# Dense stages in token blocks of 512, 256 and 288 columns instead of three of 352, and norms in pieces of at most 352

## The chip, the cores and the metric

The kernel runs on one core of one Trainium2 chip, as a single launch. The time is the device time of that launch in microseconds (us). The kernel before was timed in three runs: 2801.63, 2805.51 and 2806.05 us, with a median of 2805.51 us. One further execution was recorded by the hardware profiler; all rows below are of that execution.

The engines carry short names: PE is TensorE's matmul, PEld its weight load, DVE is VectorE, ACT is ScalarE, POOL is GpSimd and SP is SyncE.

## The reference

The kernel computes one step of a two-layer encoder trunk over 1056 tokens: 1024 of a prompt and 32 of a sample. The model width is 1024 and the hidden width of the feed-forward part is 2816.

```python
def rms_norm(x, g):
    y = xf * lax.rsqrt(jnp.mean(xf * xf, axis=-1, keepdims=True) + EPS)
    return (y * g.astype(jnp.float32)).astype(x.dtype)
...
    g = z @ w_glu + b_glu                     # end of the first mixer (S5)
    out = g[..., :D_MODEL] * jax.nn.sigmoid(g[..., D_MODEL:])
...
def conv_ffn(xn, conv_state, w_up, conv_w, conv_b, w_down):
    h = xn @ w_up
    a, bv = h[..., :D_FF], h[..., D_FF:]
    padded = jnp.concatenate([conv_state.astype(a.dtype), a], axis=1)
    c = conv_b + sum(conv_w[j] * padded[:, j:j + t] for j in range(CONV_W))
    out = (jax.nn.gelu(c) * bv) @ w_down
```

Each layer is x += mixer(rmsnorm(x)), then x += conv_ffn(rmsnorm(x)). The mixer of layer 0 is a diagonal state-space layer with a gated linear unit behind it. The mixer of layer 1 is an attention in which an indexer selects 256 keys for each query; it ends in a projection with attn_w_o.

## The kernel before

From the load of x into feature-major form on, the residual stays in one tile `xt`, with features on the 128 partitions and tokens along the columns. The input of a product is held in two float32r parts, `xh` and `xl`, whose sum is the normed value; each weight tile is likewise split into `whi` (by ACT, L143) and `wlo` (by DVE, L144). A product is therefore three matmuls for each tile of 128 features: L164 (whi times xh), L165 (whi times xl) and L166 (wlo times xh). The weight tile of 128x128 is the stationary operand, and the tokens are the moving columns. PSUM's tile for one product takes at most 512 columns.

The program's stages, with their places in the span, are the first mixer's recurrence (0 to 255 us), its gated linear unit `glu` (to about 473), `ffn` of layer 0 (to about 1244), the index scores, masks and projections of the second mixer (to about 1620), the attention (to about 1914), `out_proj` (to about 2022), and `ffn` of layer 1 with `store_block` (to the end). The stages with feature-major products, glu, out_proj and both ffn, are called the dense stages here. They cut the 1056 tokens in three blocks of `BLK = 352` columns, so that each weight tile meets each part of the input in three matmuls of 352 columns: 2688 in each of L164 to L166 for glu, the up products and out_proj, and 1056 in each for the down products, 11232 in all.

Between two stages stands the norm. `norm_block(b)` is called as soon as block b of `xt` is final, for each of three blocks in three places: glu to ffn 0, ffn 0 to the second mixer, and out_proj to ffn 1. ACT squares the eight feature tiles, DVE and POOL add them up (L193, L197), PE sums over partitions (L202, matmuls of one column), DVE forms the mean and, in some eleven small instructions, its inverse root (L173 to L178). PE then spreads that root over the partitions (L215), and DVE multiplies `xt` by it and by the gain (L218, eight times), ACT copies out `xh`, and DVE (five) and POOL (three) subtract for `xl` (L220). A product of the next stage can start on block b when these tiles are there.

Each engine works through its own list of instructions in order, and waits at semaphores for the others. A scheduler sets these lists when the kernel is built: it puts PE's norm instructions among the products of the neighbouring blocks, in the old stage and the new. If the instruction next in PE's list is L215 and DVE has not finished the root, PE waits, and the products behind it wait too.

`store_block(b)` turns the final `xt` of a block into rows of tokens: eight transposes on PE (L250), two copies on ACT (L251) and one DMA from SP for each tile of up to 128 tokens, with two `yrow` buffers. The blocks end at 352, 704 and 1056, so the tiles are 3, 3, 3 and the sample's one.

Of the kernel before, what the change touches and what calls it, by code (L numbers as in the profile page):

```python
# [23 lines left out]
BLK = 352  # L24
NB = T // BLK
# [24 lines left out]
class Trunk:  # L50
    """Shared tiles and helpers; the residual lives in xt[feature % 128, feature // 128, token]."""
# [43 lines left out]
    def load_vectors(self, pool):  # L95
        """Per-feature vectors, one column of 128 features each."""
# [34 lines left out]
    def weight(self, view, pool=False):  # L131
        """view [128, n] (rows on partitions): its two exact parts, as stationary operands; pool: split by the Pool engine."""
# [14 lines left out]
    def weight_rows(self, view, sh):  # L147
        """weight of a view whose rows lie apart."""
# [10 lines left out]
    def product(self, ps, terms):  # L159
        """ps += sum over (wh, wl, xh, xl) of w^T x, in float32 accuracy."""  # L160
# [8 lines left out]
    def rsqrt(self, y, m, tmp, iters=3):  # L169
        """y = m ** -0.5 elementwise; tmp: like y."""  # L170
# [9 lines left out]
    def norm_block(self, b, gname, g0):  # L180
        """xh/xl[:, :, block b] = parts of rmsnorm(xt) * gain."""
        nc = self.nc
        sl = slice(b * BLK, (b + 1) * BLK)
        # sums of squares, some tiles by the Pool engine
        acc = {}
        PA = (1, 3, 5)
        for k in range(KD):
            e = k in PA
            tag = "nsq" if e in acc else f"nacc{int(e)}"
            sq = self.sm.tile([P, BLK], F32, tag=tag, name=tag, bufs=self.nq if tag == "nsq" else 1)  # L190
# [9 lines left out]
        for j, o in enumerate(range(0, BLK, P)):  # L200
            n = min(P, BLK - o)
            nc.tensor.matmul(ps[:n, j : j + 1], acc[:, o : o + n], self.ones, start=True, stop=True)  # L202
        ms = self.sm.tile([P, 3], F32, tag="nms", name="nms")
        rs = self.sm.tile([P, 3], F32, tag="nrs", name="nrs")
        tm = self.sm.tile([P, 3], F32, tag="ntm", name="ntm")
        nc.vector.memset(ms, 1.0)
        for j, o in enumerate(range(0, BLK, P)):
            n = min(P, BLK - o)
# [4 lines left out]
        for j, o in enumerate(range(0, BLK, P)):  # L213
            n = min(P, BLK - o)
            nc.tensor.matmul(pb[:, o : o + n], rs[:n, j : j + 1].to_broadcast([n, P]), self.ident[:n, :n], start=True, stop=True)  # L215
        for k in range(KD):
            xn = self.sm.tile([P, BLK], F32, tag="nxn", name="nxn", bufs=self.nx)
# [21 lines left out]
    def store_block(self, pool, b):  # L239
        """y rows of block b."""  # L240
# [3 lines left out]
        e = min((b + 1) * BLK, TP)  # L244
        for o, n in [(o, min(P, e - o)) for o in range(b * BLK, e, P)] + ([(TP, TS)] if b == NB - 1 else []):
# [9 lines left out]
    def exp(self, pool, dst, x):  # L255
        """dst = exp(x) to float32 accuracy (range reduction, polynomial, exponent bits)."""
# [19 lines left out]
    def cmul(self, pool, orr, oi, xr, xi, yr, yi):  # L276
        """(orr + i oi) = (xr + i xi)(yr + i yi); shapes [.., s, n] already broadcast alike."""
# [44 lines left out]
    def ssm_params(self, pool, tmp, ld):  # L322
        """State-major tables of the discretized recurrence: partition = (re n | im n). The norm's gain is part of the inputs' taps."""
# [19 lines left out]
        # th = 2 pi k + (r + rl)  # L343
# [21 lines left out]
        # powers a^0 .. a^8  # L365
# [6 lines left out]
        # f = (a - 1) / lambda  # L372
# [22 lines left out]
        # rows to be transposed: 0-7 (Re af | Re af), 8-15 (-Im af | Im af), 16-23 (Re a | Re a),  # L395
        # 24-31 (-Im a | -Im a), 32 |a|^8, 33 state
# [24 lines left out]
        # turns per chunk of 8 tokens, in three parts  # L421
# [16 lines left out]
        # stationary rows (group | group): [0] parts 0 and 1, less a small shift; [1] part 0; [2] parts 1 and 2  # L438
# [13 lines left out]
        # input and output maps, state-major  # L452
# [63 lines left out]
        # the sample's rows take the place of b, c and the powers, which are of no more use  # L516
# [13 lines left out]
    def ssm(self):  # L530
        """xh + xl = gelu(S5(rmsnorm(x))), feature k*128 + g*16 + q at [q*8 + g, k]."""
        nc, I, O = self.nc, self.I, self.O
        C = 133  # chunk columns: 128 of the prompt, the sample's start state, 4 of the sample
        with ExitStack() as ctx:
# [34 lines left out]
            G0 = (0, 3, 6)  # groups are worked on three at a time  # L569
# [3 lines left out]
            def taps(o):  # L573
                """Input taps a^(7-j) f B, output taps C a^d, and |a|^8 of 8 groups."""
# [23 lines left out]
            def maps(o, d):  # L598
                """Within-chunk operands: inputs to state (re | im | re), inputs to outputs."""
# [25 lines left out]
            def angles(o, s):  # L625
                """cos and sin of the state's turns up to each chunk; the groups' inputs, [(j, cin), chunk]."""
# [1103 lines left out]
```

## Time and profile before

| | before |
|---|---|
| runs | 2801.63, 2805.51, 2806.05 us |
| median | 2805.51 us |
| span of the profiled execution | 2799.6 us |
| PE busy in the span | 2582.2 us (92%) |
| PEld busy | 2473.0 us (88%) |
| DVE busy | 1640.5 us (59%) |
| ACT busy | 976.6 us (35%) |
| POOL busy | 448.1 us (16%) |

The span runs from the first to the last instruction of the profiled execution; the runs' median lies 5.9 us above it. A busy share is an average over all stages, and a busy PE is not PE at its peak, since a matmul's record includes time in which the next one is already under way. A matmul's cost in a row of matmuls is therefore read from one start to the next, not from its mean duration.

### The profile page before, as it was taken

To read this page: it belongs to the slowest core of one execution; us is meant where nothing else is said; L and a number is where in the kernel's file an instruction comes from. 1 tells how busy PE (TensorE), PEld (TensorE's weight loads), DVE (VectorE), ACT (ScalarE), POOL (GpSimd) and SP (SyncE) were. 2 spreads that over 40 slices of the span, in tenths; PEclk is the share of its full clock that TensorE was granted. 3 is DMA by queue.
4 is the path that set the end of the run, shared out by engine and by line. 5 is a ranking of instruction groups with operands and counts; after the bars stand their busy time and mean duration, and the time that the engine had idled before them with its cause. 6 is when DMAs were issued, how large, how long until landed. Compare 5 with 4: busy or idle time off the path is not lost. (4 is left out here: it accounts for less than half of the span.)

```text
span 2799.6 us, 43287 instructions
## 1 busy us (share of the span) xinstructions
PE 2582.2 (92%) x17203; PEld 2473.0 (88%) x17203; DVE 1640.5 (59%) x3487; ACT 976.6 (35%) x1947; POOL 448.1 (16%) x696
## 2 busy tenths in 40 slices
PE   2887999999999999997986689999999999999999
PEld 2676999999999999996886667778999999999998
DVE  8886225644444444478799977663554444444443
ACT  4565213311111111134544466773331111111112
POOL 4672001100000000012144243220110000000000
PEclk9998999999999999998998889999999999999999
DMA  4334211111111111110121211212111111111111
GB/s 94 60 59 109 80 46 46 46 46 46 46 46 46 46 46 46 46 37 14 48 66 47 69 40 25 52 27 69 46 46 46 46 46 46 46 46 46 46 38 63
DMA packets 220662, 140.29 MB, mean 50 GB/s; under 512 B 50429, under 2 KB 212261, under 8 KB 220461
## 3 DMA queue, kind: packets, MB, share of 16 engines
q1 hardware_dynamic: 216733, 130.90, 17.0%
q10 hardware_dynamic: 3728, 6.64, 0.7%
q8 instruction: 135, 2.21, 0.3%
q14 instruction: 66, 0.54, 0.1%
HBM read 112.68 MB, written 13.40 MB: 45 GB/s over the span
## 5 line engine op out<-in xcount | busy, mean ns | idle before, releaser
L164 PE MATMUL ps_mm<-xh,whi 128*128 128x352 f32 x2688 | 870.4, 324 | 5.0 <-ACT whi L143 5.0
L166 PE MATMUL ps_mm<-xh,wlo 128*128 128x352 f32 x2688 | 869.6, 324 | 0.0
L165 PE MATMUL ps_mm<-xl,whi 128*128 128x352 f32 x2688 | 868.6, 323 | 0.0
L164 PEld LDWEIGHTS ps_mm<-xh,whi 128*128 128x128 f32 x2688 | 506.5, 188 | 5.3 <-ACT whi L143 5.2
L165 PEld LDWEIGHTS ps_mm<-xl,whi 128*128 128x128 f32 x2688 | 506.3, 188 | 0.0
L166 PEld LDWEIGHTS ps_mm<-xh,wlo 128*128 128x128 f32 x2688 | 506.0, 188 | 0.2 <-DVE wlo L144 0.2
L144 DVE TENSOR_TENSOR wlo<-wraw,whi 128x1024 fp32r<-128x1024 f32 (+1 forms) x145 | 175.5, 1222 | 416.4 <-ACT whi L143 416.4
L143 ACT CAST whi<-wraw 128x1024 fp32r<-128x1024 f32 (+1 forms) x145 | 149.9, 1047 | 712.1 <-PE ps_mm L165 702.3
L1603 DVE TENSOR_TENSOR xt<-xt,ps_mm 128x352 f32<-128x352 f32 x528 | 269.4, 520 | 191.5 <-PE ps_mm L166 191.4
L164 PE MATMUL ps_mm<-hh,whi 128*128 128x352 f32 x1056 | 341.0, 323 | 1.5 <-DVE xt L1603 1.5
L165 PE MATMUL ps_mm<-hl,whi 128*128 128x352 f32 x1056 | 340.9, 323 | 0.0
L166 PE MATMUL ps_mm<-hh,wlo 128*128 128x352 f32 x1056 | 340.7, 323 | 0.0
L1584 POOL COPY tails<-a 128x2 f32<-128x2 f32 x44 | 39.8, 904 | 1229.5 <-ACT a L1573 1229.5
L772 PE MATMUL ps_mm<-whi,xh 128*128 128x256 f32 (+3 forms) x560 | 165.8, 297 | 42.5 <-ACT raw L1217 42.5
L164 PEld LDWEIGHTS ps_mm<-hh,whi 128*128 128x128 f32 x1056 | 198.4, 188 | 2.1 <-DVE xt L1603 2.0
L166 PEld LDWEIGHTS ps_mm<-hh,wlo 128*128 128x128 f32 x1056 | 198.4, 188 | 0.0
L165 PEld LDWEIGHTS ps_mm<-hl,whi 128*128 128x128 f32 x1056 | 198.4, 188 | 0.0
L1591 DVE TENSOR_TENSOR c<-c,ps_mm 128x352 f32<-128x352 f32 (+2 forms) x176 | 71.5, 428 | 159.2 <-PE ps_mm L166 112.6
L774 PE MATMUL ps_mm<-whi,xl 128*128 128x256 f32 (+3 forms) x560 | 163.6, 293 | 0.0
L773 PE MATMUL ps_mm<-wlo,xh 128*128 128x256 f32 (+3 forms) x560 | 163.6, 293 | 0.0
L772 PEld LDWEIGHTS ps_mm<-whi,xh 128*128 128x128 f32 (+1 forms) x560 | 106.4, 190 | 47.4 <-ACT raw L1217 41.2
L1573 ACT COPY a<-ps_mm 128x352 f32<-128x352 f32 (+2 forms) x176 | 61.9, 378 | 242.1 <-PE ps_mm L166 242.0
(420 smaller groups left out, 3992.4 us busy)
## 6 DMA issues: line engine op xcount, KB each, us to landing
wraw<-in_ffn_w_up_dram SPq DMA_DIRECT2D x88, 512.0 KB
wraw<-in_ffn_w_down_dram SPq DMA_DIRECT2D x44, 512.0 KB
wraw<-in_ssm_w_glu_dram SPq DMA_DIRECT2D x128, 64.0 KB
wraw<-in_attn_w_in_dram SPq DMA_DIRECT2D x14, 512.0 KB
zo<-yo SPq DMA_DIRECT2D x64, 66.5 KB
xcm<-in_x_prompt_dram SPq DMA_DIRECT2D x8, 512.0 KB
cps<-cp SPq DMA_DIRECT2D x16, 256.0 KB
xrow<-in_x_prompt_dram ACTq DMA_DIRECT2D x8, 512.0 KB
```

The lines of the kernel that those rows point to most:

```text
L143: nc.scalar.copy(hi, raw)
L144: nc.vector.tensor_sub(lo, raw, hi.bitcast(F32))
L164: nc.tensor.matmul(ps, wh, xh, start=(i == 0), stop=False)
L165: nc.tensor.matmul(ps, wh, xl, start=False, stop=False)
L166: nc.tensor.matmul(ps, wl, xh, start=False, stop=(i == n - 1))
L772: self.nc.tensor.matmul(ps, xh, hi[:, c, a:b], start=(k == 0), stop=False)
L773: self.nc.tensor.matmul(ps, xh, lo[:, c, a:b], start=False, stop=False)
L774: self.nc.tensor.matmul(ps, xl, hi[:, c, a:b], start=False, stop=(k == KD - 1))
L1573: nc.scalar.copy(u["a"][:, co + 2 : co + 2 + n], ps[:, to - b * BLK : to - b * BLK + n])
L1584: nc.gpsimd.tensor_copy(tails[:, u["f"], 0:2], u["a"][:, TP : TP + 2])
L1591: nc.vector.tensor_mul(h, h, bv[:, to - b * BLK : to - b * BLK + n])
L1603: nc.vector.tensor_add(self.xt[:, m, blocks[b]], self.xt[:, m, blocks[b]], ps[:, :BLK])
```

## The change

The width of a block is no longer one number. `BLOCKS` lists the start and the width of each: 512, 256 and 288 columns. All dense stages take their columns from it. `norm_block(b)` now calls `norm_piece` for each of ceil(n / 352) equal pieces of the block: two of 256 columns for the first block, and one each for the others, so that a norm has four pieces instead of three. The tiles for the mean and its root have four columns instead of three. The stored tiles are 4, 2, 2 and 1.

```diff
-BLK = 352
-NB = T // BLK
+BLOCKS = [(0, 512), (512, 256), (768, 288)]
+NB = len(BLOCKS)
+BMAX = max(n for _, n in BLOCKS)
+NORM = 352
...
     def norm_block(self, b, gname, g0):
+        b0, n = BLOCKS[b]
+        c = -(-n // NORM)
+        for i in range(c):
+            self.norm_piece(b0 + i * n // c, n // c, gname, g0)
+
+    def norm_piece(self, b0, BLK, gname, g0):
         nc = self.nc
-        sl = slice(b * BLK, (b + 1) * BLK)
+        sl = slice(b0, b0 + BLK)
+        parts = [(j, o, min(P, BLK - o)) for j, o in enumerate(range(0, BLK, P))]
...
-            sq = self.sm.tile([P, BLK], F32, tag=tag, name=tag, bufs=self.nq if tag == "nsq" else 1)
+            sq = self.sm.tile([P, NORM], F32, tag=tag, name=tag, bufs=self.nq if tag == "nsq" else 1)[:, :BLK]
...
-        ms = self.sm.tile([P, 3], F32, tag="nms", name="nms")
+        ms = self.sm.tile([P, 4], F32, tag="nms", name="nms")
...
     def store_block(self, pool, b):
-        e = min((b + 1) * BLK, TP)
-        for o, n in [(o, min(P, e - o)) for o in range(b * BLK, e, P)] + ([(TP, TS)] if b == NB - 1 else []):
+        b0, n = BLOCKS[b]
+        e = min(b0 + n, TP)
+        for o, n in [(o, min(P, e - o)) for o in range(b0, e, P)] + ([(TP, TS)] if b == NB - 1 else []):
...
     def glu(self, after_block):
-                for b in range(NB):
-                    sl = slice(b * BLK, (b + 1) * BLK)
+                for b, (b0, BLK) in enumerate(BLOCKS):
+                    sl = slice(b0, b0 + BLK)
...
     def out_proj(self, after_block):
-            sl = slice(b * BLK, (b + 1) * BLK)
+            b0, BLK = BLOCKS[b]
+            sl = slice(b0, b0 + BLK)
...
     def ffn(self, layer, after_block, pool=None):
-        blocks = [slice(b * BLK, (b + 1) * BLK) for b in range(NB)]
+        blocks = [slice(o, o + n) for o, n in BLOCKS]
...
-                ps = self.ps()
-                self.product(ps[:, :BLK], [(w[0][:, k], w[1][:, k], self.xh[k][:, blocks[b]], self.xl[k][:, blocks[b]]) for k in range(KD)])
-                return ps[:, :BLK]
+                ps = self.ps()[:, : BLOCKS[b][1]]
+                self.product(ps, [(w[0][:, k], w[1][:, k], self.xh[k][:, blocks[b]], self.xl[k][:, blocks[b]]) for k in range(KD)])
+                return ps
```

The number of products does not change: 3744 matmuls of each of three widths where 11232 of one width stood. In the changed kernel the lines of `product` are L166 to L168, and the norm's two PE lines are L210 (sum over partitions) and L221 (spread of the root).

The scheduler's lists change around the norms. On PE, from glu to ffn 0 of the kernel before, the spread of block 1 has the sum of block 2 behind it (nrs is the root, nacc the sum of squares; xh, xl and whi, wlo are the parts of a product's operands):

```order
L164 MATMUL ps_mm<-xh,whi 128x352
L165 MATMUL ps_mm<-xl,whi 128x352
L215 MATMUL ps_aux<-ident,nrs 128x128 x2
L215 MATMUL ps_aux<-ident,nrs 128x96
L202 MATMUL ps_aux<-ones,nacc_4342 128x1 x2
L202 MATMUL ps_aux<-ones,nacc_4342 96x1
L166 MATMUL ps_mm<-xh,wlo 128x352
L164 MATMUL ps_mm<-xh,whi 128x352
```

The two products of 352 columns ahead of the spread, like those behind it, are some of the many that lie between the norm's rows here: 103 between the spreads of blocks 0 and 1, and 64 between those of blocks 1 and 2. In the kernel after, on PE at the same transition, this is the spread of the first block's second piece, with the sum of block 1 behind it:

```order
L166 MATMUL ps_mm<-xh,whi 128x288
L167 MATMUL ps_mm<-xl,whi 128x288
L168 MATMUL ps_mm<-xh,wlo 128x288
L221 MATMUL ps_aux<-ident,nrs 128x128 x2
L210 MATMUL ps_aux<-ones,nacc_4282 128x1 x2
L166 MATMUL ps_mm<-xh,whi 128x512
L167 MATMUL ps_mm<-xl,whi 128x512
L168 MATMUL ps_mm<-xh,wlo 128x512
```

Between the first piece's spread and this one stand 37 products of 288 columns, all of the old stage; the products of 512 columns behind it are the new stage's first, 30 of them up to the next spread and 47 from there to the last.

On DVE, at the same transition, the norm's wide instructions stand like this behind the first root (nxn is the normed tile, nms the mean, sg the gate of the old stage). Before:

```order
L178 SCALAR_TENSOR_TENSOR nrs<-ntm,nrs 128x3
L206 MEMSET nms 128x3
L218 SCALAR_TENSOR_TENSOR nxn<-xt,vec,ps_aux 128x352 x2
L220 TENSOR_TENSOR xl<-nxn,xh 128x352
L759 SCALAR_TENSOR_TENSOR sg<-ps_mm,vec,sg 128x352
L218 SCALAR_TENSOR_TENSOR nxn<-xt,vec,ps_aux 128x352 x2
L760 TENSOR_TENSOR xt<-xt,sg 128x352
L220 TENSOR_TENSOR xl<-nxn,xh 128x352
```

After:

```order
L214 MEMSET nms 128x4
L224 SCALAR_TENSOR_TENSOR nxn<-xt,vec,ps_aux 128x256 x2
L216 TENSOR_SCALAR nms<-ps_aux 128x1 x2
L202 TENSOR_TENSOR nacc_4282<-nacc_4282,nsq 128x256
L226 TENSOR_TENSOR xl<-nxn,xh 128x256
L175 TENSOR_SCALAR nrs<-nms 128x4
L224 SCALAR_TENSOR_TENSOR nxn<-xt,vec,ps_aux 128x256 x2
L176 TENSOR_SCALAR nrs<-nrs 128x4
```

The second piece's mean and root stand among the first piece's wide multiplications, and the sum of block 1's squares (nacc_4282) is already being formed there.

## Rows read from the trace of the kernel before

**Rows 1.** The page's head and its first part.

```profile
span 2799.6 us, 43287 instructions
PE 2582.2 (92%) x17203; PEld 2473.0 (88%) x17203; DVE 1640.5 (59%) x3487; ACT 976.6 (35%) x1947; POOL 448.1 (16%) x696
```

**Rows 2.** Costliest groups: line, engine, form, count | busy us, mean ns | idle before, releaser.

```profile
L164 PE MATMUL ps_mm<-xh,whi 128*128 128x352 f32 x2688 | 870.4, 324 | 5.0 <-ACT whi L143 5.0
L164 PE MATMUL ps_mm<-hh,whi 128*128 128x352 f32 x1056 | 341.0, 323 | 1.5 <-DVE xt L1603 1.5
```

**Rows 3.** Windows: length, then PE, PEld, DVE, ACT, POOL busy (count), clock, DMA share, GB/s.

```profile
455.00:560.00 105.00, 101.81 (x640) 100.39 (x639) 72.91 (x171) 42.05 (x86) 18.33 (x29) 1.00 0.14 41
560.00:1215.00 655.00, 655.00 (x4087) 655.00 (x4086) 305.26 (x489) 130.65 (x224) 23.74 (x72) 1.00 0.15 46
```

**Rows 4.** Timeline of PE, matmuls of other widths: start, duration, form [idle before].

```profile
1300.21 0.31 PE L773 MATMUL ps_mm<-wlo,xh 128*128 128x328 f32 x1
1302.93 0.31 PE L773 MATMUL ps_mm<-wlo,xh 128*128 128x328 f32 x1
...
1368.73 0.28 PE L772 MATMUL ps_mm<-whi,xh 128*128 128x256 f32 x1
1370.73 0.28 PE L774 MATMUL ps_mm<-whi,xl 128*128 128x256 f32 x1
...
1384.20 0.39 PE L938 MATMUL ps_mm<-kh,q 128*128 128x512 f32 x1
1386.73 0.39 PE L939 MATMUL ps_mm<-kl,q 128*128 128x512 f32 x1
...
1391.06 0.28 PE L772 MATMUL ps_mm<-whi,xh 128*128 128x256 f32 x1
1394.80 0.28 PE L772 MATMUL ps_mm<-whi,xh 128*128 128x256 f32 x1
```

**Rows 5.** Timeline of PE, the spreads of the root, three blocks at three transitions.

```profile
466.04 0.49 PE L215 MATMUL ps_aux<-ident,nrs 128*128 128x128 f32 x2 [1.08 <-DVE nms L206]
486.36 0.46 PE L215 MATMUL ps_aux<-ident,nrs 128*128 128x128 f32 x2 [0.99 <-DVE nms L206]
498.26 0.49 PE L215 MATMUL ps_aux<-ident,nrs 128*128 128x128 f32 x2
...
1237.58 0.88 PE L215 MATMUL ps_aux<-ident,nrs 128*128 128x128 f32 x6 [0.95 <-DVE nms L206]
1252.24 0.60 PE L215 MATMUL ps_aux<-ident,nrs 128*128 128x128 f32 x3 [0.62 <-DVE nrs L178]
1268.53 0.80 PE L215 MATMUL ps_aux<-ident,nrs 128*128 128x128 f32 x6
...
1998.98 0.49 PE L215 MATMUL ps_aux<-ident,nrs 128*128 128x128 f32 x2 [0.74 <-DVE nms L206]
2015.78 0.57 PE L215 MATMUL ps_aux<-ident,nrs 128*128 128x128 f32 x3 [0.87 <-DVE nrs L178]
2030.41 0.57 PE L215 MATMUL ps_aux<-ident,nrs 128*128 128x128 f32 x3 [0.28 <-DVE nrs L178]
```

**Rows 6.** Groups by form on DVE, 255 to 560 us, columns as in Rows 2.

```profile
L218 DVE SCALAR_TENSOR_TENSOR nxn<-xt,vec,ps_aux 128x352 f32<-128x352 f32 x24 | 13.1, 574 | 3.4 <-PE ps_aux L215 2.4 <-POOL xl L220 0.9
L144 DVE TENSOR_TENSOR wlo<-wraw,whi 128x1024 fp32r<-128x1024 f32 x10 | 12.2, 1223 | 20.0 <-ACT whi L143 20.0
L1591 DVE TENSOR_TENSOR c<-c,ps_mm 128x352 f32<-128x352 f32 x6 | 3.1, 516 | 1.6 <-ACT c L1581 1.2 <-PE ps_mm L166 0.3
L1591 DVE TENSOR_TENSOR c<-c,ps_mm 128x32 f32<-128x32 f32 x3 | 0.5, 182 | 0.0
```

**Rows 7.** Timeline of the end, PE and ACT.

```profile
2789.44 3.73 PE L250 MATMUL ps_mm<-ident,xt 128*128 128x128 f32 x32
...
2793.94 1.06 ACT L251 COPY yrow<-ps_mm 64x512 f32<-64x512 f32 x2 [1.77 <-DMA out_y_prompt_dram<-yrow]
2795.23 1.05 ACT L251 COPY yrow<-ps_mm 32x512 f32<-32x512 f32 x2 [0.23 <-DMA out_y_prompt_dram<-yrow]
```

More of the change, by code (lines that the diff above doesn't have):

```diff
@@ L199, in norm_block @@
         ps = self.ps("aux")
-        for j, o in enumerate(range(0, BLK, P)):
-            n = min(P, BLK - o)
+        for j, o, n in parts:
             nc.tensor.matmul(ps[:n, j : j + 1], acc[:, o : o + n], self.ones, start=True, stop=True)
-        ms = self.sm.tile([P, 3], F32, tag="nms", name="nms")
-        rs = self.sm.tile([P, 3], F32, tag="nrs", name="nrs")
-        tm = self.sm.tile([P, 3], F32, tag="ntm", name="ntm")
+        ms = self.sm.tile([P, 4], F32, tag="nms", name="nms")
+        rs = self.sm.tile([P, 4], F32, tag="nrs", name="nrs")
+        tm = self.sm.tile([P, 4], F32, tag="ntm", name="ntm")
         nc.vector.memset(ms, 1.0)
-        for j, o in enumerate(range(0, BLK, P)):
-            n = min(P, BLK - o)
+        for j, o, n in parts:
             nc.vector.tensor_scalar(ms[:n, j : j + 1], ps[:n, j : j + 1], 1.0 / D, EPS, op0=ALU.mult, op1=ALU.add)
@@ L212, in norm_block @@
         PX = (1, 3, 5)
-        for j, o in enumerate(range(0, BLK, P)):
-            n = min(P, BLK - o)
+        for j, o, n in parts:
             nc.tensor.matmul(pb[:, o : o + n], rs[:n, j : j + 1].to_broadcast([n, P]), self.ident[:n, :n], start=True, stop=True)
         for k in range(KD):
-            xn = self.sm.tile([P, BLK], F32, tag="nxn", name="nxn", bufs=self.nx)
+            xn = self.sm.tile([P, NORM], F32, tag="nxn", name="nxn", bufs=self.nx)[:, :BLK]
             nc.vector.scalar_tensor_tensor(xn, self.xt[:, k, sl], self.col(gname, g0 + k), pb[:, :BLK], op0=ALU.mult, op1=ALU.mult)
@@ L787, in open_spares @@
         for tag, *parts in rooms:
-            t = self.sm.tile([P, BLK], F32, tag=tag, name="room", bufs={"nsq": self.nq, "nxn": self.nx}.get(tag, 1))
+            t = self.sm.tile([P, NORM], F32, tag=tag, name="room", bufs={"nsq": self.nq, "nxn": self.nx}.get(tag, 1))
             o = 0
@@ L1542, in ffn @@
         AW = T + 4
-        blocks = [slice(b * BLK, (b + 1) * BLK) for b in range(NB)]
-        cuts = [[(b * BLK, BLK, b * BLK)] for b in range(NB - 1)] + [[(2 * BLK, TP - 2 * BLK, 2 * BLK), (TP + 2, TS, TP)]]
+        blocks = [slice(o, o + n) for o, n in BLOCKS]
+        cuts = [[(o, n, o)] for o, n in BLOCKS[:-1]] + [[(BLOCKS[-1][0], TP - BLOCKS[-1][0], BLOCKS[-1][0]), (TP + 2, TS, TP)]]
         with ExitStack() as ctx:
@@ L1572, in conv_in @@
                 for co, n, to in cuts[b]:
-                    nc.scalar.copy(u["a"][:, co + 2 : co + 2 + n], ps[:, to - b * BLK : to - b * BLK + n])
+                    nc.scalar.copy(u["a"][:, co + 2 : co + 2 + n], ps[:, to - BLOCKS[b][0] : to - BLOCKS[b][0] + n])
             def conv(u, c0=0, c1=AW - 2):
@@ L1590, in gate @@
                     hh, hl = u["hh"][:, to : to + n], u["hl"][:, to : to + n]
-                    nc.vector.tensor_mul(h, h, bv[:, to - b * BLK : to - b * BLK + n])
+                    nc.vector.tensor_mul(h, h, bv[:, to - BLOCKS[b][0] : to - BLOCKS[b][0] + n])
                     nc.scalar.copy(hh, h)
@@ L1600, in down @@
                 ms = slice(m * P, (m + 1) * P)
-                ps = self.ps()
-                self.product(ps[:, :BLK], [(u["wd"][0][:, ms], u["wd"][1][:, ms], u["hh"][:, blocks[b]], u["hl"][:, blocks[b]]) for u in us])
-                nc.vector.tensor_add(self.xt[:, m, blocks[b]], self.xt[:, m, blocks[b]], ps[:, :BLK])
+                ps = self.ps()[:, : BLOCKS[b][1]]
+                self.product(ps, [(u["wd"][0][:, ms], u["wd"][1][:, ms], u["hh"][:, blocks[b]], u["hl"][:, blocks[b]]) for u in us])
+                nc.vector.tensor_add(self.xt[:, m, blocks[b]], self.xt[:, m, blocks[b]], ps)
             pend = [start(0), start(1)]
```

2 lines of the change are left out of this document (1 added, 1 removed).

## The prediction

> **What bounds the kernel now.** I read the page's first part, then its costliest groups, then windows over single stages, then the timeline around the norms and at the end. PE is busy for 92% of the span and no other engine for more than 59% [rows 1]. The two groups of L164 are of matmuls of 352 columns [rows 2]; with their like in L165 and L166 these are 11232 instructions, and their mean record of 324 ns overlaps the next one. So the pace has to come from a stage: in the window from 560 to 1215 us PE is busy without a gap at a clock of 1.00, the upper of its two levels (2.4 GHz), while DVE is busy for 305 of 655 us [rows 3]. There 4087 matmuls take 655 us, or 160.3 ns each. In such a stretch only PE's pace per column counts. In the window from 455 to 560 us, which holds a transition, PE loses 3.2 us [rows 3], and the spreads of the root (L215) wait for DVE about 1 us at a time [rows 5]. There DVE's norm counts.
>
> So the change has three terms: the pace of 3744 triples, the waits at three transitions, and the end.
>
> **The pace.** Three matmuls of 352 columns take 3 x 160.3 = 480.9 ns. In their place come one each of 512, 256 and 288, the same 1056 columns. At 2.4 GHz 352 columns alone are 146.7 ns, so each of the 352s carries 13.6 ns beside its columns. The question is what the other widths carry, and the second mixer runs some of them at the same kind of operands:
> - 512: 11 steps in 2.53 us, 230.0 ns [rows 4], or 16.7 beside 213.3. In this stretch other work stands between, so it may be high. With the 352's own 13.6 it would be 226.9. I take the middle, 228.5.
> - 256: 33 steps in 3.74 us, 113.3 ns, in a settled run, and 17 steps in 2.00 us, 117.6 ns, just after an interruption [rows 4]. The changed kernel puts 256 between the other widths, in runs of 6 (down) or 24 (up, glu, out_proj). I take 115, nearer the settled one.
> - 288: not in the trace. 328 columns run at 18 steps in 2.72 us, 151.1 ns [rows 4]; less 40 columns that is 134.4. The 352's less 64 columns is 133.6, which I take. A straight line between 256 settled and 352 would give 129.0, but the same line gives 148.6 at 328, where the trace has 151.1, so it is a floor.
>
> The sum is 228.5 + 115 + 133.6 = 477.1 ns, 3.8 less than before, and over 3744 triples -14.2 us. The bounds: with each width high (230.0, 117.6, 134.4) it is 482.0, or +4 us; with 226.9, 113.3 and 133.6 it is 473.8, or -27 us; and with 129.0 as well 469.2, or -44 us, which the 328 speaks against. The weight loads are as many as before and lie beside the matmuls; a settled 256 shows that one of that length still covers its load.
>
> The Trainium skill bears on this term: "TensorE: Matmul & The Clock Gate", in its section on why a step is 56 ns and not 53.3, says that the cost beyond the columns is fixed, about 2.5 ns for a matmul when warm. By that the three sums would be equal and the term nothing. This trace shows another cost at 352 (13.6 ns), and a smaller one at 256 than at 352 (6.6), so the rule is not followed here, and I go by the rows.
>
> **The waits at the transitions.** A fourth piece adds a full set of the norm's small instructions at each of three places; the wide ones are 256 or 288 columns instead of 352 but more in number, and their fixed part is paid 12 times instead of 9. Worse, the order puts less PE work between some spreads. Between two spreads PE has its listed products, and DVE its listed instructions, up to the next root; whichever ends last sets the step.
>
> For DVE I count its instructions between two roots and price each by its mean [rows 6], with their overlap of some 0.08 us taken off: a wide one of 352 columns at 0.49 (L218) or 0.44, and 1.04 ns less for each column fewer ((516 - 182) / 320), the weight's low part (L144) at 1.14, and a small one at 0.14, below the 0.18 of the 32-column row. So priced, DVE has, between the spreads of blocks 0, 1 and 2:
> - before: 16.7 and 10.4 us at glu, 13.4 and 12.2 at ffn 0's end, 13.2 and 12.1 at out_proj's;
> - after, three intervals each: 12.1, 8.5, 11.1; 10.6, 10.8, 6.9; 12.1, 10.0, 6.8.
>
> PE's listed products are, before, 103 and 64 of 352 columns at glu (16.5 and 10.3 us), and 10.0 and 10.1 at ffn 0's end, 14.3 and 12.7 at out_proj's. After, with the widths above (72-column projections put at the settled 256's pace, an estimate): 37 of 288 are 4.9, 30 of 512 are 6.9 and 47 of 512 are 10.8 us at glu; 7.8, 9.2 and nothing at ffn 0's end (the last spread follows its sum at once); 11.6, 8.8 and 7.6 at out_proj's.
>
> Before, the steps between the spreads took 20.3 and 11.9 us, 14.7 and 16.3, 16.8 and 14.6 [rows 5]: 94.6 us in all for 73.9 us of PE work, so 20.7 us in which PE waited or ran at a lower clock. The longer of PE and DVE sums to 79.7 us; a step took some 2.5 us more than the longer of the two, since the chain through ACT, PE and DVE does not run side by side perfectly. After, the longer of the two sums to 89.7 us for 67.6 of PE work. If every step still has 2.5 us on top, PE loses 44.6 us instead of 20.7, a cost of 24; with none on top it loses 22.1, a cost of 1. I take the middle, +13 us, half of it at the first transition, where 12.1 us of DVE's stand against 4.9 of PE's. Nothing hides this: what waits behind the L221 on PE is all that is left of the old stage, or the first products of the new one.
>
> **The end.** The last stage makes 9 tiles of rows instead of 10, which is 8 transposes on PE fewer at 3.73 / 32 = 0.117 us, or -0.9 us [rows 7]. Before, the last block's copies wait 1.77 us and then 0.23 for a DMA to free a row buffer [rows 7]; now the last block has three tiles instead of four for two buffers, so one such wait is left. I take -2 us in all, between 0 (the DMAs end as late) and -3.
>
> **The sum.** -14.2 + 13 - 2 = -3.2 us on a profiled span of 2799.6, so 2796.4. The median of the runs lies 5.9 us above that span, and I take that distance as unchanged: 2802 us.
>
> **The rivals.**
> - The pace pays in full: a matmul carries 6.7 ns for every 256 columns begun, 6.7 at 256, 13.3 at 288, 352 and 512. For it: 256 settled carries 6.6, the 352 13.6, the 328 14.4. Against it: the 512's 230.0. The triple is then 226.7 + 113.3 + 133.3 = 473.3, or -28 us; with +13 and -2 this is -17, 2788 us.
> - The transitions win (slower): the 512s stay at 230.0 and the 256s do not settle between the other widths, 230.0 + 116 + 133.6 = 479.6, so the pace gives only -5 us, and each of the nine steps keeps its 2.5 us on top, +24. With the end this is +17, 2822 us; at half of that excess, 2813. For it: the 512's measured pace, and that PE's work between the spreads at glu falls to 4.9 us in one step. It decides as soon as the pace gives less than what the waits take, that is below 3 ns for a triple if the waits cost 13 us.
> - The pace doesn't change at all: equal columns, equal time, 480.9. Then the transitions and the end are all, +11, 2816 us. Against it: 256 and 352 differ in the trace by 47 ns for 96 columns, which 2.4 GHz makes 40.
>
> **How the numbers follow.** A measurement of this kernel can tell 0.2%, some 5.6 us, from no change. The forecast has 0.45 (between -14 and +6), the full pace 0.20, the winning transitions 0.30 and the unchanged pace 0.05. Of the forecast's own range of 2791 to 2812 about two fifths lie below -5.6, half within 5.6 and a tenth above: 0.19, 0.22 and 0.04. The full pace is all faster; the winning transitions are slower but for 0.04 within; the unchanged pace is slower. That makes faster 0.39, same 0.26 and slower 0.35. The range reaches from 2784, the full pace with the waits at 9 us, to the winning transitions at 2822.
>
> **What would show it.** Right: in a window within ffn, 512, 256 and 288 run at 228, 115 and 134 ns from start to start, and the three sum to 477; L221's idle time by DVE rises from about 1 us to several at glu's second piece, and PE's idle time there from 3 us to about 10. Wrong: a sum outside 473 to 480 ns for three, a transition in which PE's products cover DVE's piece, or an end that isn't shorter. The forecast falls if one of the two large terms is off by half: the pace alone shifts the time by 3.7 us for each ns of a triple.

## The result: 1% slower, and the profile after

The changed kernel takes 2831.9 us (median of 4 runs, 2830.8 to 2834.7) against 2805.8 us in the same series: 26.1 us more, and a ratio of 1.0101, with a 95% interval of 1.0089 to 1.0113. The forecast was 2802. Below, a difference in us is one between medians, unless traces or ratios are named; the ratios can differ from it by some 2 us. The page of the changed kernel begins:

```profile
span 2829.8 us, 43415 instructions
PE 2595.7 (92%) x17195; PEld 2318.5 (82%) x17195; DVE 1650.5 (58%) x3577; ACT 982.5 (35%) x1993; POOL 454.5 (16%) x711
```

PE's share is the same 92% as in [rows 1], so it says nothing here. What tells is where the 30.2 us between the two profiled spans arise. To see it, I took the start of that matmul with which a given share of all dense columns is done, in both traces, and the difference of the two at each share:

| stretch | the difference grows by | forecast |
|---|---|---|
| up to the first product | 0.8 us | 0 |
| glu's, ffn 0's and ffn 1's middle (pace) | 0.6 + 3.4 + 3.5 = 7.5 us | -14.2 |
| glu to ffn 0 | 10.4 us | |
| ffn 0 to the second mixer, and through it | 11.5 us | |
| out_proj to ffn 1 | 1.6 us | |
| the three transitions together | 23.5 us | +13 |
| the end | -1.6 us | -2 |

The spans differ by 4 us more than the medians do: the changed kernel's own execution has 1.75 us around its span, so the one profiled of before, with a span of 2799.6, was most likely the quickest of its runs (2801.63). The 5.9 us between span and median that the prediction took as unchanged belonged to that one execution: in the changed kernel they are 2.1.

Of the 11.5 us from ffn 0 to the second mixer, 10.5 are there by the first index scores, so they arise at the transition. How sure the entries are is shown by the later runs with the same norms in the same order (edge_only, good_after, shifted, widths, places and places2, below): the first transition is 10.3 to 10.8 us there and the third 1.5 to 1.7, but the second 11.5 to 14.5. In runs with the norms of before (mid_only, mid_264, good_place and bad_place) the second lies at -0.5 to +3.9 us. So it is known to some 4 us, and the other two to 0.5.

In the window of a settled ffn, the changed kernel has fewer matmuls in the same 655 us than the 4087 of [rows 3], and in that of the first transition PE is busy for 94.6 us, not 101.8, and its clock falls to 0.93 (columns as in [rows 3]):

```profile
455.00:560.00 105.00, 94.64 (x579) 84.47 (x578) 68.14 (x185) 43.51 (x98) 22.60 (x34) 0.93 0.13 39
560.00:1215.00 655.00, 655.00 (x4064) 594.77 (x4063) 309.57 (x501) 129.08 (x222) 23.50 (x70) 1.00 0.15 45
```

The timeline of PE in the changed kernel shows the four spreads at each transition that answer to the three of [rows 5] (start, duration, then the idle time before it in brackets):

```profile
470.89 0.71 PE L221 MATMUL ps_aux<-ident,nrs 128*128 128x128 f32 x4 [0.90 <-DVE nrs L180]
485.32 1.01 PE L221 MATMUL ps_aux<-ident,nrs 128*128 128x128 f32 x3 [8.38 <-DVE nms L214]
497.32 0.63 PE L221 MATMUL ps_aux<-ident,nrs 128*128 128x128 f32 x4
509.48 0.71 PE L221 MATMUL ps_aux<-ident,nrs 128*128 128x128 f32 x4
...
1256.10 0.68 PE L221 MATMUL ps_aux<-ident,nrs 128*128 128x128 f32 x4 [0.51 <-DVE nms L214]
1269.86 0.56 PE L221 MATMUL ps_aux<-ident,nrs 128*128 128x128 f32 x1
1283.69 0.50 PE L221 MATMUL ps_aux<-ident,nrs 128*128 128x128 f32 x3
1293.51 0.80 PE L221 MATMUL ps_aux<-ident,nrs 128*128 128x128 f32 x2 [8.72 <-DVE nrs L180]
...
2031.20 0.71 PE L221 MATMUL ps_aux<-ident,nrs 128*128 128x128 f32 x4 [1.21 <-DVE nms L214]
2044.42 0.68 PE L221 MATMUL ps_aux<-ident,nrs 128*128 128x128 f32 x4 [0.48 <-DVE nms L214]
2055.86 0.71 PE L221 MATMUL ps_aux<-ident,nrs 128*128 128x128 f32 x4
2064.77 0.49 PE L221 MATMUL ps_aux<-ident,nrs 128*128 128x128 f32 x3
```

The two long waits of 8.4 and 8.7 us stand at the two places of the order where PE had least to do: 37 products at glu's second piece, and nothing behind the last sum at ffn 0's end. The nine steps between these spreads add up to 109.6 us.

The first of these waits also costs clock. PE stands still from 476.9 to 485.3 us, and from 479 to 493 us the granted clock is 0.51, the lower of its two levels. The last row is of the kernel before, whose clock stays at 1.00 through this transition (columns as in [rows 3] and [rows 5]):

```profile
479.00:493.00 14.00, 6.86 (x20) 5.22 (x21) 11.78 (x35) 6.40 (x18) 5.32 (x9) 0.51 0.17 55
489.07 0.63 PE L168 MATMUL ps_mm<-xh,wlo 128*128 128x512 f32 x1
489.49 0.63 PE L166 MATMUL ps_mm<-xh,whi 128*128 128x512 f32 x1
489.92 0.63 PE L167 MATMUL ps_mm<-xl,whi 128*128 128x512 f32 x1
...
466.00:500.00 34.00, 31.93 (x204) 31.09 (x204) 29.90 (x80) 18.30 (x37) 9.51 (x12) 1.00 0.11 32
```

A 512 there follows the one before it after 0.43 us instead of 0.23. Between 10.2% and 13% of the dense columns the changed kernel takes 10.5 us more (10.4 by the marks of the table): PE idles for 9.2 us instead of 2.0, and its busy time grows by 3.3, most of it at that lower clock. At ffn 0's end the clock falls in both kernels; from 1225 to 1320 us it is 0.87 before and 0.80 in the changed kernel.

For the pace, here is PE's timeline of the changed kernel, first products of the runs of 24 in the up stage, then those of the runs of 6 in the down stage:

```profile
602.58 0.28 PE L166 MATMUL ps_mm<-xh,whi 128*128 128x256 f32 x1
...
605.40 0.29 PE L166 MATMUL ps_mm<-xh,whi 128*128 128x288 f32 x1
...
608.57 0.39 PE L166 MATMUL ps_mm<-xh,whi 128*128 128x512 f32 x1
...
614.14 0.28 PE L166 MATMUL ps_mm<-xh,whi 128*128 128x256 f32 x1
...
640.45 0.40 PE L166 MATMUL ps_mm<-hh,whi 128*128 128x512 f32 x1
...
643.37 0.40 PE L166 MATMUL ps_mm<-hh,whi 128*128 128x512 f32 x1
```

In the up stage 24 of each width take 2.82, 3.17 and 5.57 us, so 117.5, 132.1 and 232.1 ns, together 481.7 for three. In the down stage six such triples take 2.92 us, 486.7 each. Before, it was 480.9 in the mean of both.

### The profile page after: what moved, and what is told of

It reads as the page before. It is cut to its first block, busy times and chain, and to the rows that moved or that the text cites. A ratio compares the mean times of both kernels' runs of the same rounds, so it can differ in the third digit from the quotient of the medians.

```text
span 2829.8 us, 43415 instructions
## 1 busy us (share of the span) xinstructions
PE 2595.7 (92%) x17195; PEld 2318.5 (82%) x17195; DVE 1650.5 (58%) x3577; ACT 982.5 (35%) x1993; POOL 454.5 (16%) x711
## 5 line engine op out<-in xcount | busy, mean ns | idle before, releaser
L166 PE MATMUL ps_mm<-xh,whi 128*128 128x256 f32 (+2 forms) x2688 | 871.1, 324 | 7.4 <-ACT whi L145 5.3
L168 PE MATMUL ps_mm<-xh,wlo 128*128 128x256 f32 (+2 forms) x2688 | 872.9, 325 | 0.0
L167 PE MATMUL ps_mm<-xl,whi 128*128 128x256 f32 (+2 forms) x2688 | 870.2, 324 | 0.0
L166 PEld LDWEIGHTS ps_mm<-xh,whi 128*128 128x128 f32 x2688 | 507.8, 189 | 46.4 <-ACT whi L145 5.5
L168 PEld LDWEIGHTS ps_mm<-xh,wlo 128*128 128x128 f32 x2688 | 506.5, 188 | 39.7 <-DVE wlo L146 0.8
L1611 DVE TENSOR_TENSOR xt<-xt,ps_mm 128x512 f32<-128x512 f32 (+2 forms) x528 | 271.3, 521 | 196.0 <-PE ps_mm L168 192.7
L167 PE MATMUL ps_mm<-hl,whi 128*128 128x256 f32 (+2 forms) x1056 | 344.7, 326 | 0.0
L168 PE MATMUL ps_mm<-hh,wlo 128*128 128x256 f32 (+2 forms) x1056 | 342.8, 325 | 0.0
L166 PE MATMUL ps_mm<-hh,whi 128*128 128x256 f32 (+2 forms) x1056 | 342.1, 324 | 0.0
L166 PEld LDWEIGHTS ps_mm<-hh,whi 128*128 128x128 f32 x1056 | 200.0, 189 | 16.6
L168 PEld LDWEIGHTS ps_mm<-hh,wlo 128*128 128x128 f32 x1056 | 199.2, 189 | 15.6
L1581 ACT COPY a<-ps_mm 128x256 f32<-128x256 f32 (+2 forms) x176 | 62.0, 378 | 264.9 <-PE ps_mm L168 264.9
L1599 DVE TENSOR_TENSOR c<-c,ps_mm 128x256 f32<-128x256 f32 (+2 forms) x176 | 71.3, 427 | 112.5 <-PE ps_mm L168 66.8
```

Source lines behind the costliest of these rows:

```text
L166: nc.tensor.matmul(ps, wh, xh, start=(i == 0), stop=False)
L167: nc.tensor.matmul(ps, wh, xl, start=False, stop=False)
L168: nc.tensor.matmul(ps, wl, xh, start=False, stop=(i == n - 1))
L1581: nc.scalar.copy(u["a"][:, co + 2 : co + 2 + n], ps[:, to - BLOCKS[b][0] : to - BLOCKS[b][0] + n])
L1599: nc.vector.tensor_mul(h, h, bv[:, to - BLOCKS[b][0] : to - BLOCKS[b][0] + n])
L1611: nc.vector.tensor_add(self.xt[:, m, blocks[b]], self.xt[:, m, blocks[b]], ps)
```

## The experiments

Two theories stood at the start. **A**: a matmul's time is a straight line over its columns, so that equal columns gain nothing, and what is lost is lost at the transitions, where a step between two spreads lasts as long as DVE's list and some 2.5 us more. The rival is the prediction's own step: the pace gains, and something else eats it.

**The middle alone, and the edges alone.** In both, ffn takes two lists of blocks, one for its middle and one for the stretches next to a norm or to the store:

```diff
+MID_UP = [(0, 512), (512, 256), (768, 288)]
+MID_DOWN = [(0, 512), (512, 256), (768, 288)]
...
-                    for b in range(NB):
+                    for b in MID_UP:
                         conv_in(u, b)
```

In mid_only `BLOCKS` is three of 352 and the middle as above; edge_only has the two exchanged.

> Blocks of 512, 256 and 288 only in the middle of both ffn stages (hidden tiles 2 to 21 up, and their down products); glu, out_proj, the norms, the first two hidden tiles, the last down products and the store keep three blocks of 352. Theory A (a matmul's time is a straight line over its columns, so equal columns take equal time, and the down products lose some 6 ns for three): +7 us, 2812 to 2814. Rival (the prediction's step: three widths take 477 ns instead of 481, and the loss is all at the norms): -12 us, 2794.

Measured: 2809.9 us against 2802.2, a ratio of 1.0026 (1.0017 to 1.0035), +7.6 us. In the traces, ffn 0's and ffn 1's middle lose 3.2 us each.

> The opposite: glu, out_proj, norms, the first two hidden tiles, the last down products and the store in 512, 256 and 288 (four norm pieces), the middle of both ffn stages in 352. Theory A (the norm's steps between spreads last as long as DVE's list plus 2.5 us, and PE has too little beside them): +22 us, about 2828, with the waits at glu's and ffn 0's end as in the changed kernel. Rival (the loss is mostly the pace of the wide blocks): under +10, 2810 to 2815.

Measured: 2825.9 us, 1.0077 (1.0064 to 1.0090), +23.6 us. The two parts add up to 31 us, close to the 30 of the profiled spans. So the pace loses 7 us where the forecast had a gain of 14, and the transitions cost nearly twice what it had.

**The same widths in another order.**

```diff
-BLOCKS = [(0, 512), (512, 256), (768, 288)]
+BLOCKS = [(0, 256), (256, 288), (544, 512)]
```

> The change with its blocks in another order: 256, 288, 512. As many norm pieces (4) and the same widths everywhere; the 512 block is the last, so more of the old stage's products lie beside the first pieces. Theory A (cover by the order: PE has 35.6, 22.8 and 34.9 us of products between the spreads instead of 22.6, 17.0 and 28.0): the transitions cost +7 instead of +23, with the pace +7: 2818 to 2822. Rival (a fourth piece costs what it costs, wherever it stands): 2830 or more.

Measured: 2818.6 us, 1.0052 (1.0038 to 1.0065), +16.4 us: 10 less than the change's +26.1 (14 by the ratios), with the same number of pieces. In its window of the first transition PE is busy for 5 us more than in the changed kernel, at a clock of 1.00:

```profile
455.00:560.00 105.00, 99.69 (x603) 87.66 (x602) 72.93 (x197) 44.76 (x102) 19.19 (x34) 1.00 0.14 41
```

In the traces its three transitions take 11.8 us, where those of the change take 23.5. So part of the transitions' price is the order, by which the widest block comes first and leaves PE the least beside its two pieces. A's time of 2818 to 2822 is met by other parts than its own: the transitions take more than its 7 us, the pace loses 3 us instead of 7, and the end, now with the widest block, takes 2.5 us longer instead of being shorter.

**Six pieces on blocks of 352.**

```diff
-        c = -(-n // NORM)
+        c = -(-n // PIECE)
```

`PIECE` is 176, and `BLOCKS` is three of 352.

> Blocks of 352 as before, each norm in two pieces of 176: six pieces at each transition, no change of any product. Theory A (each step is DVE's list plus up to 2.5 us, products between spreads 39.8, 20.5 and 40.4 us): +24 to +39 us, 2830 to 2845. Rival (the number of pieces costs nothing on PE as long as a whole old block stands beside them; only the 512 block's late end hurts): within 4 us of before, 2802 to 2810.

Measured: 2843.4 us, 1.0142 (1.0128 to 1.0155), +41 us, at the upper end of A's range (+24 to +39 us, 2830 to 2845). Pieces cost by themselves: nine more of them cost 4.6 us apiece, though no product has changed.

**A shorter root.** In the changed kernel, `self.rsqrt(rs, ms, tm)` became `self.rsqrt(rs, ms, tm, 1)`.

> The changed kernel, with one step of Newton's iteration instead of three for the norm's root, so the root is less exact: 6 small DVE instructions fewer, some 1.0 us, in each of 12 pieces. Theory A (DVE's list sets all nine steps between spreads and part of the first): -9 to -12 us, 2820 to 2823. Rival (DVE's small instructions lie in its waits for ACT and PE): 0 to -3 us, 2829 to 2832.

Measured: 2822.3 us, 1.0070 (1.0055 to 1.0086). By the ratios that is 9 us less than the change, and at glu's second piece, where PE waited 8.38 us, it now waits 2.41 (PE's timeline, the spreads behind the first piece's):

```profile
474.10 0.71 PE L221 MATMUL ps_aux<-ident,nrs 128*128 128x128 f32 x4 [2.41 <-DVE nrs L180]
485.06 0.61 PE L221 MATMUL ps_aux<-ident,nrs 128*128 128x128 f32 x4
495.94 0.94 PE L221 MATMUL ps_aux<-ident,nrs 128*128 128x128 f32 x6
```

DVE's small instructions lie on the path, as A has it, but not in all nine steps alike: in the traces 6.8 us of the gain arise at glu's end, 1.0 at ffn 0's (within that stretch's scatter) and 0.5 at out_proj's.

**Less on DVE, more on POOL.** In the kernel before, `PX = (1, 3, 5)` became `PX = (1, 3, 5, 7)`.

> The kernel before, with four instead of three of each norm's subtractions for xl on POOL (feature tiles 1, 3, 5 and 7), so DVE has one wide instruction of about 0.44 us less in each of 9 norms. Theory A (the step between spreads is DVE's list): -0.44 us in each of 4 to 6 steps, -2 to -3 us, 2799 to 2804. Rival (the chain of engines sets the step, and POOL's 1.0 us for the last tile comes late): 0 to +3 us.

Measured: 2811.6 us, 1.0031 (1.0019 to 1.0042), +8 us. A's forecast for this fell, and so did the rival's size, though not its sign: in the traces, 4 us are lost at glu's end, 3 at ffn 0's (within that stretch's scatter) and 2 at out_proj's. At glu's end the second spread waits 2.29 us instead of the 0.99 of [rows 5], and right behind it PE is busy without a gap at a clock of 0.57:

```profile
487.00:495.00 8.00, 8.00 (x35) 8.00 (x36) 5.50 (x15) 2.19 (x5) 1.91 (x2) 0.57 0.01 2
```

35 matmuls at 160.3 ns would be 5.6 us, so some 2.4 of the 4 us are clock and the step itself is only 0.8 us longer. That the way of the last tile through POOL makes it longer fits, but is not shown by itself.

**The fixed part of a matmul.** Four blocks of 264 in the middle of both ffn, with the two lists of mid_only:

> Blocks of 352 at the norms and edges as before, but the middle of both ffn stages in four blocks of 264 columns: 11520 matmuls of 264 in place of 8640 of 352. Theory A (3.3 ns and 0.446 ns a column): four take 484.5 ns instead of 481, over 2880 such groups +10 us, 2812 to 2817. Rival (the prediction's step, 13.6 ns fixed for every matmul): 494.4, +39 us, 2841 to 2846.

Measured: 2822.2 us, 1.0068 (1.0054 to 1.0081), +19 us, between the two. The window counts:

```profile
560.00:1215.00 655.00, 655.00 (x5374) 655.00 (x5374) 316.52 (x598) 133.44 (x257) 24.01 (x70) 1.00 0.15 46
```

655 us / 5374 are 121.9 ns, four of them 487.5: 6.6 ns over three of 352, and over 2880 groups 19 us. A matmul more costs some 6.6 ns here (5.3 to 7.9 by the interval of the ratio), neither A's 3.3 nor the forecast's 13.6. The blocks of 264 also begin at other columns, which turns out below to matter, so this is not a fixed part alone.

**Widths by themselves.** Behind the last store of the changed kernel, products with nothing beside them (the first line is repeated for 256, 288, 352, 256 and 448 columns):

```diff
+                go(lambda p, w, x, d: mm(p, w, x, **d), 0, 512, 4)
...
+                for i in range(48):
+                    mm(ps[:, :512], z[:, (i % 8) * P : (i % 8 + 1) * P], z[:, 0:512], start=(i == 0), stop=(i == 47))
```

> The changed kernel with matmuls added behind its last store, where no other engine works: the products' pattern (whi on xh, whi on xl, wlo on xh over eight feature tiles) at 512, 256, 288, 352, 256 and 448 columns in 4 runs of 24 each; 512, 256, 288 by turns in runs of 6; 48 times one pair of operands at 512 and at 256; 48 with tokens stationary and weights moving at 512 and 256; 48 with zeros moving at 512 and 256; 48 with zeros on both sides at 512. Their results are not used, so only the trace counts. Theory A (a straight line, 3.3 ns and 0.446 ns a column, that belongs to the matmul itself): 232, 117.5, 132, 160.5 and 203 ns, by turns the same, 481 for the three. Rival 1 (the dense stages' 117.5 at 256 comes of neighbours or of other engines, and alone it settles at the 113.3 of the second mixer; 226.9 at 512): three sum to 474. Rival 2 (a fixed 13.6 ns for each): 227, 120, 133.6, 160.3, 200. If the values that pass through matter, the zeros are faster than the others at the same width.

Measured, from start to start: 231.8, 117.6, 132.5, 160.9, 117.5 and 201.8 ns, the same as in the dense stages, so other engines have no part in it; by turns 233.5, 117.0 and 131.5, together 482. The runs of 48 stand on PE's timeline as one row each (start, length; divided by 48 from one row's start to the next):

```profile
2929.31 11.37 PE L1678 MATMUL ps_mm<-xh,whi 128*128 128x512 f32 x48
2940.52 5.82 PE L1681 MATMUL ps_mm<-xh,whi 128*128 128x256 f32 x48
2946.17 11.21 PE L1684 MATMUL ps_mm<-whi,xh 128*128 128x512 f32 x48
2957.22 5.62 PE L1687 MATMUL ps_mm<-whi,xh 128*128 128x256 f32 x48
2962.67 11.36 PE L1692 MATMUL ps_mm<-hl,whi 128*128 128x512 f32 x48
2973.86 5.76 PE L1695 MATMUL ps_mm<-hl,whi 128*128 128x256 f32 x48
2979.46 11.07 PE L1698 MATMUL ps_mm<-hl 128*128 128x512 f32 x48
```

One pair of tiles takes 233.5 ns at 512 and 117.7 at 256; with tokens stationary and weights moving it is 230.2 and 113.5. That is the 113.3 of [rows 4], which the prediction took for "settled": there, too, the weights move and the tokens are stationary, the other way round than in the dense products. The 117.6 of [rows 4] is from the same lines, so neither was a reading of the dense operands. Zeros moving are no faster (233.1 and 116.7), so the moving values do not matter. In the last run, with zeros on both sides and both in one tile, the 512 takes some 227; which of the two makes it quicker, this run can't tell, but places may. The quickest seen, 113.3 at 256 and 227 at 512, are both 17/16 of the columns at 2.4 GHz; a 352 would be 155.8 at that rate, and the 160.3 of [rows 3] has 4.5 ns more. No run of 352 settled at 155.8.

The Trainium skill ("TensorE: Matmul & The Clock Gate", "Wait — 56ns, not 53.3ns?") has 2.5 ns beside the columns, 215.7 at 512. No step of 512 columns in these traces was under 224. What follows from it for this change, equal time for equal columns in equal numbers of matmuls, holds for the up products (481.7 against 481.7 by their own means); its figure does not.

**Other places for hh and hl.**

```diff
-                u["hh"] = fp.tile([P, T], F32R, tag="hh", name="hh", bufs=4)
+                u["hh"] = fp.tile([P, T + 24], F32R, tag="hh", name="hh", bufs=4)[:, :T]
```

`hl` is changed alike.

> The changed kernel with the two tiles hh and hl (moving operands of the down products) made 24 columns longer, the added columns unused: the same instructions, other places in SBUF. Theory P (each matmul loses 0 to 10 ns by the places of its operands, and the down products drew bad ones in this layout): the three widths of the down products leave 486 ns by more than 1 ns, either way, and single steps of the six in a run change by several; the up products stay at 482. Rival (short runs of 6, or the values of hh and hl): the down products stay at 486 within 0.5, and the time at 2831 to 2833.

Measured: 2827.8 us, 1.0086 (1.0069 to 1.0103). That is 4 us less than the change by the ratios. The down products take 482.8 ns for three instead of 486.3 by their means, the up products the same 481.9. Theory P holds, and the rival falls: no instruction was changed.

**Which places.**

```diff
+                for o in range(64):
+                    ps = self.ps()
+                    for k in range(KD):
+                        for h, x in ((0, self.xh), (0, self.xl), (1, self.xh)):
+                            mm(ps[:, :352], wd[h][k], x[k][:, o : o + 352], start=(k == h == 0 and x is self.xh), stop=(k == KD - 1 and h == 1))
```

These lines are of places2, which repeats the pattern of a product at one first column after the other; places does so with single pairs.

> The changed kernel with matmuls added behind its last store, results unused: one pair of tiles repeated, the moving one's first column shifted by 8 columns and by 1 column at a time, then the stationary one shifted by 16, at 352, 256 and 512 columns. Only the trace counts. Theory P: the step changes with the shift between 155.8 ns (17/16 of 352 columns at 2.4 GHz) and some 165, with a pattern that comes back at a fixed distance, and alike at every repetition. Rival (the loss belongs to the width): 160.5 at every shift, within 1 ns.

Measured: at 352 columns a step (the mean of five) moves between 157.4 and 166.8 ns with the moving tile's first column, and in shifts of 8 columns the row of values comes back after 64 columns, within 0.5 ns but for the first round, all along the 640 columns tried. Shifting the stationary tile moves it by some 2 ns at most. At 256 columns the same pair, weights stationary as in the dense products, takes 113.2 to 113.4 ns at first column 64 and at every 64th from there on, and 117 to 119 at the others tried, column 0 among them (118.0): the 113.3 of [rows 4] can be had with dense operands too, at the right place.

> The changed kernel with the products' pattern added behind its last store, results unused: runs of 24 over eight feature tiles (whi on xh, whi on xl, wlo on xh) at 352 columns, with the moving tiles' first column shifted from 0 to 63 in steps of one; then at 512 and 256 in steps of four; then 24 on hh and hl at 352, shifted from 0 to 63. Only the trace counts. Theory P (the place of the moving operand within 64 columns decides): the mean of a run of 352 moves with the shift over more than 2 ns, between 158 and 163, and there are shifts at which the whole pattern is faster than the 160.5 of the dense stages. Rival (over eight tiles the places average out): 160.5 within 0.7 at every shift, so nothing is to be had from moving a tile.

Measured: the mean of a run on xh and xl is 158.6 to 165.3 ns. PE's timeline at the start of five runs, begun 1 to 5 columns late:

```profile
2828.49 0.32 PE L1662 MATMUL ps_mm<-xh,whi 128*128 128x352 f32 x1
...
2832.42 0.33 PE L1662 MATMUL ps_mm<-xh,whi 128*128 128x352 f32 x1
...
2836.32 0.32 PE L1662 MATMUL ps_mm<-xh,whi 128*128 128x352 f32 x1
...
2840.17 0.32 PE L1662 MATMUL ps_mm<-xh,whi 128*128 128x352 f32 x1
...
2844.02 0.32 PE L1662 MATMUL ps_mm<-xh,whi 128*128 128x352 f32 x1
```

The runs begun at 1, 2, 3 and 4 take 3.93, 3.90, 3.85 and 3.85 us. Over all 64 shifts the means for first columns 0, 1, 2 and 3 of every four are 160.6, 163.9, 162.5 and 159.5 ns on xh and xl, and 160.2, 163.4, 162.4 and 159.3 on hh and hl. Four columns are 16 bytes; the Trainium skill ("SBUF — State Buffer", "Specifications (TRN2)") gives 16-byte lines, each crossing of which has a price, and this trace agrees as far as the repetition by four in these means goes. Which of the four first columns begins a line, and what the slower repetition by 64 columns is, no run here shows.

**The place as a change of its own.** The kernel before, with the moving tiles' first column chosen from those runs; bad_place has 1 in the place of both 7 and 15, with PE's list the same in both, and the same as before:

```diff
-                self.xh.append(self.xp.tile([P, T], F32R, tag="xh", name="xh", bufs=KD))
+                self.xh.append(self.xp.tile([P, T + 8], F32R, tag="xh", name="xh", bufs=KD)[:, 7 : 7 + T])
...
-                u["hh"] = fp.tile([P, T], F32R, tag="hh", name="hh", bufs=4)
+                u["hh"] = fp.tile([P, T + 16], F32R, tag="hh", name="hh", bufs=4)[:, 15 : 15 + T]
```

`hl` is changed alike.

> The kernel before (three blocks of 352, the same instructions in the same order on PE), with xh begun 7 columns and hh and hl 15 columns later in tiles made 8 and 16 columns longer; xl stays, since there is no room. Theory P (the place of the moving operand decides; in the shifted runs 159.0 instead of 160.7 at 7 and 39, 158.0 instead of 160.1 at 15 and 47): -1.6 ns on 5376 matmuls and -2.1 on 2112, and -1 on the 1056 that hl and wlo share, together about -13 to -15 us, 2788 to 2793. Rival (in the whole kernel the places average out): within 3 us of before.

Measured: 2798.0 us against 2802.1, 0.9982 (0.9974 to 0.9991), -4 to -5 us. It is the one version here that beats both kernels. The window, with 4105 matmuls where before had 4087 [rows 3]:

```profile
560.00:1215.00 655.00, 655.00 (x4105) 654.90 (x4103) 306.40 (x493) 132.63 (x228) 23.61 (x72) 1.00 0.16 46
```

That is 159.6 ns for 160.3. The forecast of -13 was too large: whi on xh went from 160.9 to 159.5 and hl from 160.1 to 158.2, but wlo on xh stayed at 160.6 and hh at 160.0. Shifts measured in one layout carry over in part only.

> The same tiles, all begun 1 column later instead, at which the shifted runs had 163.9 and 163.3 ns. Theory P: +3.2 ns on 5376 matmuls and +3.5 on 3168, +25 to +30 us, 2828 to 2836, with not an instruction more and PE's order unchanged against good_place. Rival: within 3 us of before.

Measured: 2824.8 us, 1.0081 (1.0066 to 1.0097), +23 us, somewhat less than the 25 to 30 expected, with 162.4 ns in the window:

```profile
560.00:1215.00 655.00, 655.00 (x4033) 655.00 (x4033) 302.89 (x488) 127.86 (x219) 22.66 (x70) 1.00 0.15 45
```

Between the two lie 27 us, and nothing but the first column of three kinds of tiles. The moving operands of those kinds take 2 to 5 ns more in the second kernel, while xl, whose place is the same in both, takes 159.4 and 159.6. The rival, that places average out, falls.

> The changed kernel with the tiles of good_place (xh 7 columns, hh and hl 15 columns later). Theory P: blocks begin at columns 0, 512 and 768, which are 0 in 64, so all three have the place of 7 or 15; the down products lose their +6 ns for three, the up products 3 to 5 ns for three: 2831.9 less 12 to 20, 2812 to 2820, and the transitions' +23 us stay. Rival: within 3 us of the changed kernel, 2829 to 2835.

Measured: 2823.4 us, 1.0075 (1.0061 to 1.0089): 7 us less than the change by the ratios, short of the 12 to 20. The down products are at 479 ns for three, below even the kernel before, the up products at 481.3; the differences at the transitions are those of the change. So the change's loss of pace was the layout of hh and hl, for the most part, and its transitions stay.

## Why the prediction was wrong

**The pace, -14 forecast, +7.5 measured.** The step that failed is "each of the 352s carries 13.6 ns beside its columns", taken as a fixed cost that the other widths might carry too or escape. Most of it grows with the columns: from 256 to 512 the dense products add 0.446 ns a column, where 2.4 GHz is 0.417, which is 10.5 ns at 352 (9.2 by the 17/16 of the quickest runs). The remaining 3 to 5 ns come with every matmul, in some more, in some less, and move with the place of the operands. The 256's 113.3, read as a settled pace, and the 117.6, read as an unsettled one, both belonged to moving weights. The dense operands run at 117.6, and in places at 113.3 or 118 by the place alone. That the second reading is the same number as theirs was not explained by any run. The high bound, 482 ns with 230.0 and 117.6, is what the up products took. The warning stood in [rows 4]: the 512's 230.0 lay 16.7 over its columns, more than the 352, where a fixed cost would be the same. For the pace, the rival in which it is unchanged came nearest. That the pace even lost 7.5 us was in no case: the 6 ns that three down products lose come from where hh and hl are read, as shifted and good_after show with PE's list unchanged.

**The transitions, +13 forecast, +23.5 measured.** The mechanism was right, and the place too, with almost half of it at the first; the signs named for it came, 8.4 us of wait at glu's second piece and 10.4 us of idle PE in its window. The size failed where the prediction took "the middle" between steps with 2.5 us on top and steps with none. With 2.5 on all nine they would have taken 89.7 + 22.5 = 112.2 us, and they took 109.6. Nothing in [rows 5] spoke for less: all six steps of before had an excess, of 1.3 to 4.1 us. The cost of 24 stood there as the upper bound and as part of the rival on the slower side, whose time of 2822 is 10 us short mainly by its pace (at half of the excess its own terms give 2811, not the 2813 stated). No term held a fall of the clock at glu's end, where [rows 3] has 1.00 and the changed kernel 0.93: of that transition's price some 3 us are busy time added behind the long wait, most of it at the lower level. small_first and halves confirm both halves of the account: fewer products beside a piece, and more pieces. How the 23.5 us divide between the two was not measured.

**The end, -2 forecast, -1.6 measured.** Right.

**The bounds.** The high bound for the pace was +4 us and that for the waits +24. With -2 they make +26, and the range ended at 2822 since each bound was used with the other term's better value. That +26 is also the difference of the medians is in part luck: the traces have +30, with the pace beyond its bound, and the 4 us between are the execution of before that happened to be profiled.

## What to carry to other kernels

Read a matmul's pace from the very operands that the change will use; another pair of the same width can be 4% quicker for a reason that has nothing to do with width. Splitting one stage into unequal blocks moves the cover at the stage's borders: count, for each step between two releases, what is listed on the engine that waits and on the engine waited for, and keep the excess that every step of before shows. Look at the granted clock behind a long wait, too: at glu's end, behind 8.4 us of it, a 512 took 426 ns instead of 232. Where two costs are bounded, add the unfavourable bounds once as well.

## What the runs showed of the hardware

The start-to-start time of these float32r matmuls with a stationary tile of 128x128 went with the moving operand's first column: at 352 columns from 157.4 to 166.8 ns, repeating by 64 columns, and in the mean by 4. The quickest runs were at 17/16 of the columns at 2.4 GHz (113.3 ns at 256, 227 at 512). It was the same in a full kernel and with all other engines at rest, and the same when zeros moved. With nothing else changed the place moved the whole kernel from 2798 to 2825 us. After PE's wait of 8.4 us the granted clock was 0.51 and a 512 took 426 ns instead of 232. How stationary and moving places work together was not settled.
